# Linear attention on one core: f32 loads with the casts moved to VectorE and ScalarE, the first group on the sync queue, ten output buffers

## The chip, the cores and the metric

The kernel runs on one core of a Trainium2 chip. The metric is the device time of one execution in microseconds (us). The kernel before takes 134.85 us (median of three runs, 134.44 to 135.09). GB/s are 10^9 bytes per second, MB 10^6 bytes.

## The reference

Inputs Q, K and V are f32 arrays of 8 batches x 12 heads x 512 positions x 64 features. Per head:

```python
Q_feat = np.maximum(0, Q) + 1
K_feat = np.maximum(0, K) + 1
KV = np.einsum('bhkd,bhkv->bhdv', K_feat, V)
K_sum = np.sum(K_feat, axis=2)
numerator = np.einsum('bhqd,bhdv->bhqv', Q_feat, KV)
denominator = np.einsum('bhqd,bhd->bhq', Q_feat, K_sum)
out = numerator / (denominator[:, :, :, None] + 1e-10)
```

Each input and the output is 12.58 MB, so 37.75 MB are read and 12.58 MB written: 50.33 MB in all. Nothing is read twice.

## The kernel before, in words

The 96 heads are taken four at a time: two "pairs" (`M = 2`), each with two heads on the 128 partitions, 64 partitions to a head and eight positions (`C = 8`) to a partition. That makes `NG = 24` groups. One group is three loads (`k_raw`, `v_raw`, `q_raw`, each 128 x 1024 elements, 0.524 MB of f32 in HBM) and one store (`o_sb`, 128 x 1024 f32, 0.524 MB). In HBM each partition's share of a load is two runs of 2,048 bytes.

A group goes through three stages, each one iteration of the main loop apart:

- `features(g)`: VectorE makes `kf` from `k_raw` and `qf` from `q_raw` (add 1, then maximum with 1), ScalarE copies `v_raw` into `v_aug`, whose 65th column holds ones, so that the sum of K_feat comes out of the same matmul.
- `kv_and_transpose(g)`: 32 matmuls into `kva_ps`, eight transposes of `qf` into `qt_ps`, both taken out of PSUM by ScalarE.
- `output(g)`: 32 matmuls into two `o_ps` tiles, then for each tile a reciprocal of the denominators and a multiplication into `o_sb`, both on VectorE.

The order is written out by hand (`tc.manual_schedule()`): each engine executes its instructions in program order. Iteration `it` issues `features(it)`, `kv_and_transpose(it - 1)`, `output(it - 2)`, then `load(it + 6)` and one store. The first six groups are loaded ahead of the loop. All loads and stores are issued from GpSimd (POOL), in one order, on the software queue; each DMA there also waits for the DMA eight places before it (the compiled program uses eight completion semaphores in turn for this queue), so at most eight are in flight. The input tiles are bf16: the DMA casts f32 to bf16 on its way, which the software queue can do.

Three sizes set the waits. `IN_BUFS = 6` input buffers: `load(it + 6)` takes the buffer that `features(it)` has read. `OUT_BUFS = 7` output buffers: `output(g)` writes the buffer that the store of group g - 7 has to have left. `LAG = 5`: the store of group s stands in iteration s + 5, behind `load(s + 11)`; after the last load (group 23) there are twelve stores in a row.

Of the kernel before, what the change touches and what calls it, by code (L numbers as in the profile page):

```python
# [1 line left out]

# [5 lines left out]

FP32 = mybir.dt.float32
BF16 = mybir.dt.bfloat16  # L10
ALU = mybir.AluOpType

BANK = 512
VP = 66
IN_BUFS = 6
OUT_BUFS = 7
LAG = 5


@with_exitstack  # L20
def kernel(
    ctx: ExitStack,
    tc: tile.TileContext,
    Q: bass.AP,
    K: bass.AP,
    V: bass.AP,
    out: bass.AP,
):

    nc = tc.nc

    B, H, S, D = Q.shape
    P = 128
    C = 8
    NPAIR = B * H * S // (P * C)
    M = 2
    NG = NPAIR // M
    D1 = D + 1  # L40

    def pview(t):
        return t.flatten_outer_dims().rearrange("(n p c) d -> p n c d", p=P, c=C)

    q_dram = pview(Q)
    k_dram = pview(K)
    v_dram = pview(V)
    o_dram = pview(out)

    const = ctx.enter_context(tc.tile_pool(name="const", bufs=1))  # L50
    in_pool = ctx.enter_context(tc.tile_pool(name="in_pool", bufs=IN_BUFS))
    feat_pool = ctx.enter_context(tc.tile_pool(name="feat", bufs=3))
    mid_pool = ctx.enter_context(tc.tile_pool(name="mid", bufs=3))
    out_pool = ctx.enter_context(tc.tile_pool(name="out_pool", bufs=OUT_BUFS))
    recip_pool = ctx.enter_context(tc.tile_pool(name="recip", bufs=4))
    psum_qt = ctx.enter_context(tc.tile_pool(name="psum_qt", bufs=2, space=bass.MemoryType.PSUM))
    psum_kva = ctx.enter_context(tc.tile_pool(name="psum_kva", bufs=1, space=bass.MemoryType.PSUM))
    psum_out = ctx.enter_context(tc.tile_pool(name="psum_out", bufs=2, space=bass.MemoryType.PSUM))

    identity = const.tile([P, P], BF16, name="identity")  # L60
    NV = 3
    v_aug = [const.tile([P, M, C, VP], BF16, name=f"v_aug{i}") for i in range(NV)]

    raw = {}
    feat = {}
    mid = {}
    outs = {}

    def load(g):
        k_raw = in_pool.tile([P, M, C, D], BF16, name="k_raw")  # L70
        v_raw = in_pool.tile([P, M, C, D], BF16, name="v_raw")
        q_raw = in_pool.tile([P, M, C, D], BF16, name="q_raw")
        sl = slice(g * M, g * M + M)
        nc.gpsimd.dma_start(out=k_raw, in_=k_dram[:, sl])  # L74
        nc.gpsimd.dma_start(out=v_raw, in_=v_dram[:, sl])  # L75
        nc.gpsimd.dma_start(out=q_raw, in_=q_dram[:, sl])  # L76
        raw[g] = (k_raw, v_raw, q_raw)

    def store(g):
        nc.gpsimd.dma_start(out=o_dram[:, g * M : g * M + M], in_=outs.pop(g))  # L80

    def features(g):
        k_raw, v_raw, q_raw = raw.pop(g)
        kf = feat_pool.tile([P, M, C, D], BF16, name="kf")
        qf = feat_pool.tile([P, C, M, D], BF16, name="qf")
        nc.vector.tensor_scalar(  # L86
            out=kf, in0=k_raw, scalar1=1.0, scalar2=1.0, op0=ALU.add, op1=ALU.max
        )
        nc.scalar.copy(out=v_aug[g % NV][:, :, :, 0:D], in_=v_raw)  # L89
        nc.vector.tensor_scalar(  # L90
            out=qf.rearrange("p c m d -> p m c d"),
            in0=q_raw,
            scalar1=1.0,
            scalar2=1.0,
            op0=ALU.add,
            op1=ALU.max,
        )
        feat[g] = (kf, qf)

    def kv_and_transpose(g):  # L100
        kf, qf = feat.pop(g)
        va = v_aug[g % NV]
        kva_ps = psum_kva.tile([P, 2, BANK], FP32, name="kva_ps")
        for c in range(C):
            for m in range(M):
                for j in range(2):
                    nc.tensor.matmul(  # L107
                        kva_ps[64 * m : 64 * m + 64, j, 0:D1],
                        lhsT=kf[64 * j : 64 * j + 64, m, c, :],
                        rhs=va[64 * j : 64 * j + 64, m, c, 0:D1],  # L110
                        start=(c == 0),
                        stop=(c == C - 1),
                    )
        kva = mid_pool.tile([P, 2, VP], BF16, name="kva")
        nc.scalar.copy(out=kva[:, :, 0:D1], in_=kva_ps[:, :, 0:D1])  # L115

        qt_ps = psum_qt.tile([P, C, P], BF16, name="qt_ps")
        for c in range(C):
            nc.tensor.transpose(qt_ps[:, c, :], qf[:, c, :, :], identity)  # L119
        qt = mid_pool.tile([P, C, P], BF16, name="qt")  # L120
        nc.scalar.copy(out=qt, in_=qt_ps)  # L121
        mid[g] = (kva, qt)

    def output(g):
        kva, qt = mid.pop(g)
        o_sb = out_pool.tile([P, M, C, D], FP32, name="o_sb")
        ops = [psum_out.tile([P, 2, BANK], FP32, tag="o_ps", name="o_ps") for _ in range(M)]
        for c in range(C):
            off = (c % 4) * D1
            for m in range(M):  # L130
                for j in range(2):
                    nc.tensor.matmul(  # L132
                        ops[m][64 * j : 64 * j + 64, c // 4, off : off + D1],
                        lhsT=qt[64 * m : 64 * m + 64, c, 64 * j : 64 * j + 64],
                        rhs=kva[64 * m : 64 * m + 64, j, 0:D1],
                        start=True,
                        stop=True,
                    )
        for m in range(M):
            cells = ops[m][:, :, 0 : 4 * D1].rearrange("p b (r x) -> p b r x", x=D1)  # L140
            recip = recip_pool.tile([P, 2, 4, 1], FP32, name="recip")
            nc.vector.reciprocal(out=recip, in_=cells[:, :, :, D:D1])  # L142
            nc.vector.tensor_tensor(  # L143
                out=o_sb[:, m].rearrange("p (b r) d -> p b r d", b=2),
                in0=cells[:, :, :, 0:D],
                in1=recip.to_broadcast([P, 2, 4, D]),
                op=ALU.mult,
            )
        outs[g] = o_sb

    with tc.manual_schedule():
        for g in range(IN_BUFS):
            load(g)
            if g == 0:
                make_identity(nc, identity)
                for t in v_aug:
                    nc.gpsimd.memset(t[:, :, :, D:VP], 1.0)  # L157
        for it in range(NG + 2):
            if it < NG:
                features(it)  # L160
            if 1 <= it < NG + 1:
                kv_and_transpose(it - 1)
            if it >= 2:
                output(it - 2)
            if it + IN_BUFS < NG:
                load(it + IN_BUFS)
            s = it - 2 - (LAG - 2)
            if s >= 0:
                store(s)
        for s in range(NG + 2 - LAG, NG):  # L170
            store(s)


# [1 line left out]
_INS = ['Q', 'K', 'V']  # L175
_OUTS = [((8, 12, 512, 64), 'float32')]


# [23 lines left out]
```

## Time and profile before

| | |
|---|---|
| time, median of three | 134.85 us |
| the profiled execution | 134.27 us, its span 132.5 us |
| DMA: moved on the SBUF side of the queue | 31.46 MB (loads count as bf16) |
| DMA: read from and written to HBM | 37.75 MB and 12.58 MB |
| POOL (with DMA issue) / VectorE / TensorE / ScalarE busy | 70.3 / 57.6 / 56.6 / 53.9 us |
| one DMA issue on POOL, load or store | 0.72 to 0.73 us |
| issue to landing, median: loads / stores | 9.7 us / 9.9 us |
| SyncE (SP) | issues nothing |

The span is the time between the first and last event that the profile has; the execution's own time has 1.8 us more around it. Busy shares are averages over the whole span. A slice of the DMA row is the share of the core's 16 DMA engines that had a packet; it can be above one, because packets overlap. GB/s in the profile count bytes on the destination side: a cast load counts half of what it reads from HBM.

### The profile page before, as it was taken

The numbers are of one execution on the slowest core, as the hardware profiler recorded it, in microseconds if no ns is written. First come the engines' busy times: TensorE is split into PE (matmuls) and PEld (weight loads), VectorE is DVE, ScalarE is ACT, GpSimd is POOL, SyncE is SP. The second block draws the span as 40 slices with busy tenths as digits, with TensorE's granted clock in tenths as the row PEclk, the third lists the DMA queues.
The fourth block names the chain that finished last, engine by engine and source line by source line (L and its number), as shares of the span: only waits on it lengthen the run. The fifth ranks groups of instructions, "written<-read, shape, count | busy, mean of one in ns | idle before, by whom it ended". The sixth has DMA issues, their size and how long they took to land.

```text
span 132.5 us, 3993 instructions
## 1 busy us (share of the span) xinstructions
PE 56.6 (43%) x1728; PEld 45.5 (34%) x1728; DVE 57.6 (43%) x144; ACT 53.9 (41%) x73; POOL 70.3 (53%) x105
## 2 busy tenths in 40 slices
PE   0041576665567400516526426336065264378200
PEld 0031355454355300505415325325054153266200
DVE  0112177555567100742733724725427347297710
ACT  3035435666364463053363362461543533625000
POOL 6995546465475546555465574653554655224220
DMA  1999999999999999999999999999999999999760
GB/s 11 193 173 192 205 206 204 205 205 205 205 209 201 208 203 286 253 238 292 230 257 291 217 271 282 214 283 268 223 283 259 232 284 251 413 412 416 299 267 25
DMA packets 23057, 31.70 MB, mean 239 GB/s; under 512 B 1537, under 2 KB 19969, under 8 KB 23041
## 3 DMA queue, kind: packets, MB, share of 16 engines
q0 software_dynamic: 23040, 31.46, 110.6%
q8 instruction: 13, 0.21, 0.6%
q14 instruction: 4, 0.02, 0.0%
HBM read 37.75 MB, written 12.58 MB: 380 GB/s over the span
## 4 chain that ended last, share of the span: by engine, by line
DMA 73%; issue 11%; POOL 6%; DVE 4%; POOLq 1%; DVEq 0%
DMA out_dram<-o_sb 45%; DMA q_raw<-in_Q_dram 22%; DMA k_raw<-in_K_dram 6%; POOL out_dram L80 3%; DVE o_sb L143 3%; POOL k_raw L74 1%; POOL q_raw L76 1%; DVE qf L90 1%; POOL v_raw L75 1%; POOLq L197 1%; DVE kf L86 1%; DVE recip L142 0%; POOL identity masks.py:199 0%; POOL identity masks.py:197 0%; POOL v_aug L157 0%
## 5 line engine op out<-in xcount | busy, mean ns | idle before, releaser
L143 DVE TENSOR_TENSOR o_sb<-o_ps,recip 128x512 f32<-128x512 f32 x48 | 33.2, 692 | 42.5 <-DMA out_dram<-o_sb 41.3
L132 PE MATMUL o_ps<-kva,qt 64*64 64x65 bf16 x768 | 21.3, 244 | 46.9 <-DVE recip L142 37.9
L89 ACT COPY v_aug<-v_raw 128x1024 bf16<-128x1024 bf16 x24 | 25.1, 1046 | 26.2 <-DMA v_raw<-in_V_dram 26.2
L132 PEld LDWEIGHTS <-qt 64*64 64x64 bf16 x768 | 15.5, 149 | 55.0 <-ACT v_aug L89 31.2
L121 ACT COPY qt<-qt_ps 128x1024 bf16<-128x1024 bf16 x24 | 24.3, 1014 | 9.6 <-PE qt_ps L119 9.6
L80 POOL DMA_DIRECT2D out_dram<-o_sb x24 | 17.6, 734 | 19.4 <-DVE o_sb L143 10.2
L74 POOL DMA_DIRECT2D k_raw<-in_K_dram x24 | 17.4, 723 | 16.5 <-DMA v_raw<-in_V_dram 4.9
L107 PE MATMUL kva_ps<-v_aug,kf 64*64 64x65 bf16 x768 | 16.0, 242 | 21.3 <-ACT kva L115 12.8
L119 PE MATMUL qt_ps<-identity,qf 128*128 128x128 bf16 x192 | 24.8, 310 | 0.0
L76 POOL DMA_DIRECT2D q_raw<-in_Q_dram x24 | 17.5, 729 | 12.1 <-DMA q_raw<-in_Q_dram 6.0
L107 PEld LDWEIGHTS <-kf 64*64 64x64 bf16 x768 | 14.6, 153 | 22.5 <-issue 22.5
L75 POOL DMA_DIRECT2D v_raw<-in_V_dram x24 | 17.3, 719 | 8.9 <-DMA v_raw<-in_V_dram 4.1
L115 ACT CAST kva<-kva_ps 128x130 bf16<-128x130 f32 x24 | 6.4, 267 | 31.9 <-PE kva_ps L107 31.9
L119 PEld LDWEIGHTS <-qf 128*128 128x128 bf16 x192 | 18.5, 141 | 1.6
L90 DVE TENSOR_SCALAR qf<-q_raw 128x1024 bf16<-128x1024 bf16 x24 | 10.4, 432 | 17.7 <-DMA q_raw<-in_Q_dram 17.7
L86 DVE TENSOR_SCALAR kf<-k_raw 128x1024 bf16<-128x1024 bf16 x24 | 10.0, 418 | 6.9 <-DMA k_raw<-in_K_dram 6.9
L142 DVE RECIPROCAL recip<-o_ps 128x8 f32<-128x8 f32 x48 | 9.7, 201 | 1.9 <-PE o_ps L132 1.4
L89 ACT ACT_TABLE_LOAD x1 | 1.3, 1283 | 0.7 <-PEq L186 0.7
masks.py:199 POOL TENSOR_SCALAR_AFFINE_SELECT identity<-identity 128x128 bf16<-128x128 bf16 x1 | 0.3, 287 | 0.1
L157 POOL MEMSET v_aug<- 128x32 bf16 x3 | 0.2, 120 | 0.0
masks.py:197 POOL MEMSET identity<- 128x128 bf16 x1 | 0.2, 231 | 0.0
L186 POOL MEMSET const-float32-0.0<- 128x1 f32 x1 | 0.1, 93 | 0.3 <-issue 0.3
(3 smaller groups left out, 0.3 us busy)
## 6 DMA issues: line engine op xcount, KB each, us to landing
out_dram<-o_sb POOLq DMA_DIRECT2D x24, 512.0 KB, 9.9
k_raw<-in_K_dram POOLq DMA_DIRECT2D x24, 256.0 KB, 9.7
v_raw<-in_V_dram POOLq DMA_DIRECT2D x24, 256.0 KB, 9.7
q_raw<-in_Q_dram POOLq DMA_DIRECT2D x24, 256.0 KB, 9.7
```

Source lines behind the costliest of these rows:

```text
L74: nc.gpsimd.dma_start(out=k_raw, in_=k_dram[:, sl])
L75: nc.gpsimd.dma_start(out=v_raw, in_=v_dram[:, sl])
L76: nc.gpsimd.dma_start(out=q_raw, in_=q_dram[:, sl])
L80: nc.gpsimd.dma_start(out=o_dram[:, g * M : g * M + M], in_=outs.pop(g))
L86: nc.vector.tensor_scalar(out=kf, in0=k_raw, scalar1=1.0, scalar2=1.0, op0=ALU.add, op1=ALU.max)
L89: nc.scalar.copy(out=v_aug[g % NV][:, :, :, 0:D], in_=v_raw)
L90: nc.vector.tensor_scalar(out=qf.rearrange("p c m d -> p m c d"), in0=q_raw, scalar1=1.0, scalar2=1.0, op0=ALU.add, op1=ALU.max,)
L107: nc.tensor.matmul(kva_ps[64 * m : 64 * m + 64, j, 0:D1], lhsT=kf[64 * j : 64 * j + 64, m, c, :], rhs=va[64 * j : 64 * j + 64, m, c, 0:D1] ...
L119: nc.tensor.transpose(qt_ps[:, c, :], qf[:, c, :, :], identity)
L121: nc.scalar.copy(out=qt, in_=qt_ps)
L132: nc.tensor.matmul(ops[m][64 * j : 64 * j + 64, c // 4, off : off + D1], lhsT=qt[64 * m : 64 * m + 64, c, 64 * j : 64 * j + 64], rhs=kva[6 ...
L143: nc.vector.tensor_tensor(out=o_sb[:, m].rearrange("p (b r) d -> p b r d", b=2), in0=cells[:, :, :, 0:D], in1=recip.to_broadcast([P, 2, 4, ...
```

## The change

Input tiles become f32, so that the loads no longer cast; the two VectorE instructions and the ScalarE copy of `features` read f32 and write bf16 as before, with unchanged code. Group 0 gets three f32 tiles of its own in a new pool (`head_pool`) and its loads are issued from SyncE (`nc.sync`, a hardware queue); all other loads and all stores remain on GpSimd. The masks and the ones columns, which GpSimd makes after the loads of group 0, are now made after the loads of group 1. There are ten output buffers in place of seven, and `LAG` goes from 5 to 3: the store of group s stands in iteration s + 3, behind `load(s + 9)`, and ten stores follow the last load.

```diff
-OUT_BUFS = 7
-LAG = 5
+OUT_BUFS = 10
+LAG = 3
...
+    head_pool = ctx.enter_context(tc.tile_pool(name="head_pool", bufs=1))
...
     def load(g):
-        k_raw = in_pool.tile([P, M, C, D], BF16, name="k_raw")
-        v_raw = in_pool.tile([P, M, C, D], BF16, name="v_raw")
-        q_raw = in_pool.tile([P, M, C, D], BF16, name="q_raw")
+        if g == 0:
+            pool, dt, eng = head_pool, FP32, nc.sync
+        else:
+            pool, dt, eng = in_pool, FP32, nc.gpsimd
+        k_raw = pool.tile([P, M, C, D], dt, name="k_raw")
+        v_raw = pool.tile([P, M, C, D], dt, name="v_raw")
+        q_raw = pool.tile([P, M, C, D], dt, name="q_raw")
         sl = slice(g * M, g * M + M)
-        nc.gpsimd.dma_start(out=k_raw, in_=k_dram[:, sl])
-        nc.gpsimd.dma_start(out=v_raw, in_=v_dram[:, sl])
-        nc.gpsimd.dma_start(out=q_raw, in_=q_dram[:, sl])
+        eng.dma_start(out=k_raw, in_=k_dram[:, sl])
+        eng.dma_start(out=v_raw, in_=v_dram[:, sl])
+        eng.dma_start(out=q_raw, in_=q_dram[:, sl])
         raw[g] = (k_raw, v_raw, q_raw)
...
         for g in range(IN_BUFS):
             load(g)
-            if g == 0:
+            if g == 1:
                 make_identity(nc, identity)
```

## The prediction

> **What bounds the kernel now.** I read the slices of the page first. The DMA row and the GB/s below it, and the traffic to HBM:
>
> ```profile
> DMA  1999999999999999999999999999999999999760
> GB/s 11 193 173 192 205 206 204 205 205 205 205 209 201 208 203 286 253 238 292 230 257 291 217 271 282 214 283 268 223 283 259 232 284 251 413 412 416 299 267 25
> ...
> HBM read 37.75 MB, written 12.58 MB: 380 GB/s over the span
> ```
>
> The DMA engines are full from the second slice to the 37th; no compute engine is busy over half of the span. The GB/s row has three levels, and a finer look at three quiet windows (us, busy times by engine, clock, DMA share, GB/s) gives them:
>
> ```profile
> core 0: us, PE busy (x) PEld busy (x) DVE busy (x) ACT busy (x) POOL busy (x), PEclk, DMA share, GB/s
> 14.00:40.00 26.00, 15.51 (x472) 12.16 (x471) 14.60 (x38) 14.04 (x21) 14.58 (x20) 1.00 1.24 205
> 66.00:96.00 30.00, 12.74 (x370) 10.18 (x368) 13.26 (x33) 13.35 (x18) 16.66 (x24) 1.00 1.19 257
> 114.00:122.00 8.00, 5.19 (x176) 4.28 (x176) 6.25 (x15) 3.92 (x6) 1.64 (x3) 1.00 1.03 415
> ```
>
> The first window holds loads alone; a cast load counts half its HBM bytes, so 205 is 410 GB/s read. The second mixes three loads and a store per group: 2.097 MB in HBM against 1.311 MB counted, so 257 x 1.6 = 411. The third is stores alone, f32 on both sides: 415. Three levels in the row are thus one speed of HBM bytes, 410 to 415 GB/s. 50.33 MB at 412 are 122 us of the 132.5; about 10 us lie at the ends. The waits show the same from the compute side:
>
> ```profile
> DVE o_sb L143 <- DMA out_dram<-o_sb: 41.3, 13, 8.7
> PE o_ps L132 <- DVE recip L142: 37.9, 14, 8.5
> ```
>
> VectorE waits 41.3 us for an output buffer that a store still holds, and TensorE waits behind it. While the queue is full this costs nothing. It does matter once the loads end, because compute is then three groups in arrears:
>
> ```profile
> 112.91 0.72 POOL L80 DMA_DIRECT2D out_dram<-o_sb  x1 [0.20 <-issue]
> 116.85 0.73 POOL L80 DMA_DIRECT2D out_dram<-o_sb  x1 [3.22 <-DVE o_sb L143]
> ...
> 124.29 0.72 POOL L80 DMA_DIRECT2D out_dram<-o_sb  x1 [1.76 <-DVE o_sb L143]
> 126.77 0.72 POOL L80 DMA_DIRECT2D out_dram<-o_sb  x1 [1.75 <-DVE o_sb L143]
> ```
>
> The last five stores leave 2.48 us apart, VectorE's pace, where a store needs 0.524 MB / 415 = 1.26 us. The windows at both ends show what is lost:
>
> ```profile
> 2.50:3.00 0.50, 0.00 (x0) 0.00 (x0) 0.00 (x0) 0.00 (x0) 0.50 (x2) 1.00 0.31 29
> 3.00:3.50 0.50, 0.00 (x0) 0.00 (x0) 0.00 (x0) 0.00 (x0) 0.50 (x1) 1.00 0.92 96
> 3.50:4.00 0.50, 0.00 (x0) 0.00 (x0) 0.00 (x0) 0.00 (x0) 0.42 (x3) 1.00 1.19 199
> ...
> 124.00:125.00 1.00, 0.65 (x30) 0.51 (x30) 0.27 (x2) 0.00 (x0) 0.71 (x1) 1.00 0.72 283
> 127.00:128.00 1.00, 0.00 (x0) 0.00 (x0) 0.00 (x0) 0.00 (x0) 0.50 (x1) 1.00 0.04 16
> ```
>
> By 4.0 us the queue has moved 0.5 x (29 + 96 + 199) = 162 kB, worth 0.8 us at 205, so it starts in effect at 3.2 us. At 127 to 128 us it stands empty, one store still to come.
>
> [...] The trace shows 1.27 (issue) to some 3 us for the first, which includes 0.84 us of issue; of SP it has nothing. [...] in the trace POOL's issue stays at 0.71 to 0.82 us.
>
> **The change part by part.**
>
> *f32 loads.* HBM bytes don't change. SBUF takes 37.75 MB in place of 18.87. No row shows an f32 load. The nearest is the f32 store, 415 against 410 for the cast load; if loads come to 415 too, 37.75 MB take 91.0 us in place of 92.1, a gain of 1.1. The other bound: writing SBUF at twice the rate costs something, say 395 GB/s, 95.6 us, +3.5. I take half of the gain, **-0.5**, because the direction of the store differs.
>
> *Casts.* The rows concerned:
>
> ```profile
> L90 DVE TENSOR_SCALAR qf<-q_raw 128x1024 bf16<-128x1024 bf16 x24 | 10.4, 432 | 17.7 <-DMA q_raw<-in_Q_dram 17.7
> L86 DVE TENSOR_SCALAR kf<-k_raw 128x1024 bf16<-128x1024 bf16 x24 | 10.0, 418 | 6.9 <-DMA k_raw<-in_K_dram 6.9
> ```
>
> [...] +0.27 each, 48 x 0.27 = +13 us of VectorE. The ScalarE copy stays at 1.05 [...]. VectorE's iteration goes from 2.48 us to 3.0, hidden under the transfers of a group: 2.097 MB / 411 = 5.1 us with stores, 1.573 / 410 = 3.84 us without. So **0**. [...]
>
> *Group 0 on SP.* Three issues leave POOL and go to SP, which has nothing else to do. POOL's first load, now of group 1, still leaves at 1.27 and would arrive as before, so the worst is 0. [...] I take **-0.9**. Three fewer DMAs pass through the eight-deep window. The masks, about 0.8 us on POOL, again follow three issues, so `identity` is ready at the same time, before the first transpose (9.0 us).
>
> *Ten output buffers and LAG 3.* `output(g)` now needs the store of group g - 10, placed in iteration g - 7, nine iterations earlier; before, store g - 7 in iteration g - 2, four earlier. At 5.1 us an iteration nine exceed the 9.9 us that a store is in flight by far, so the 41.3 us wait goes, and compute follows the landing loads. What is late next is the loads: harmless, as the queue is full. The store of group s stands behind the load of q for group s + 9, which waits for `qf` of group s + 3; VectorE does that after `o_sb` of group s. So the earlier store adds no wait on POOL, and the loads behind it aren't held up.
>
> At the end: let T be the landing of q_raw of group 23. Stores 14 to 20 are ready, 7 x 1.26 = 8.8 us of transfer. VectorE still owes groups 21 to 23: `qf` 0.7, then two reciprocals and two multiplications, 1.75, so 21 is ready at T + 2.4; 22 follows at about T + 4.2 and 23, behind transposes (1.04), ScalarE (1.01) and matmuls, at about T + 6.5. The queue needs them from T + 8.8 on. It never runs dry. Before, the store of group 12 had landed when VectorE went on at 115.02; eleven were left, 5.77 MB, 13.9 us at 415: 128.9. The last really landed at 126.77 + 3.2 (the shortest issue-to-landing of a store) = 130.0. So **-1.1**. The close after it, 132.5 - 130.0 = 2.5 us, stays.
>
> *Sum:* -0.5 + 0 - 0.9 - 1.1 = -2.5: a span of 130.0, 131.8 us for an execution like the profiled one (134.27), which is 0.6 below the median; set against the median of 134.85, **132.3 us**.
>
> **The rivals.**
>
> *A (0.60):* the sum above, 132.3; its own range 130.5 to 133.9.
>
> *B (0.22), the other side:* f32 loads are slower, since SBUF is written at twice the rate. For it: no transfer in this trace writes SBUF above 210 GB/s. Against it: stores move 415 through the same engines. The ends are worth 2.0 us, so it decides where 92.1 us of loads become 94.1, below 401 GB/s; at 395 the time is 134.85 + 3.5 - 2.0 = 136.3. A third of this case lies within 0.5%.
>
> *C (0.13):* only the tail is saved: SP's first packets come no earlier, or share the engines with GpSimd's such that the head's dips (174 and 150 GB/s between 6 and 9 us) grow; loads run at 410. 134.85 - 1.1 = 133.8. Two thirds of it still count as faster.
>
> *D (0.05):* VectorE becomes the bound. [...]
>
> **How the numbers follow.** Changes under 0.5% can't be told from none. Faster: A, and 0.09 of C: 0.69. Same: 0.04 of C, 0.07 of B, 0.02 of D: 0.13. Slower: 0.15 of B and 0.03 of D: 0.18. The range, 130.0 to 136.0, takes in the lower end of A with loads a little above 415, and B down to about 396 GB/s.
>
> **What would show it.** Right: load-only windows near 415 GB/s counted in f32; no wait of the multiplication on a store; `kf` and `qf` at 0.69; a first `kf` about 1 us before 5.11; DMA share near one until the last store, which leaves before the queue is dry. Wrong: load-only windows below 400, stores leaving 2.5 us or more apart at the end, or POOL issues well over 0.8 us with DMA gaps after them.

## The result and the profile after

The changed kernel takes 136.15 us (median of four runs, 135.90 to 136.72) against 134.81 for the kernel before: a ratio of 1.011, 95% interval 1.006 to 1.015. It is slower, by 1.3 us, where 2.5 us of gain was forecast, and 136.15 lies just outside the range.

The slices of the changed kernel, its hardware and software queues, and the traffic to HBM:

```profile
DMA  3999999999999999999999999999999999999960
GB/s 114 385 395 387 387 385 386 385 383 386 386 382 390 399 401 396 403 402 403 403 397 403 398 404 407 393 403 405 398 399 410 397 402 407 398 413 412 386 276 12
...
q0 software_dynamic: 13392, 48.76, 93.4%
q1 hardware_dynamic: 816, 1.57, 3.2%
...
HBM read 37.75 MB, written 12.58 MB: 375 GB/s over the span
```

The engines are still full from end to end, but now every byte counts once, and the row reads directly in HBM bytes. There is no level at 410 to 415 until the stores stand alone, in the slices with 413 and 412; the prediction's own sign of being wrong, load-only windows below 400, is there. Two windows, loads alone and loads mixed with stores (us, busy times by engine, clock, DMA share, GB/s):

```profile
14.00:34.00 20.00, 12.82 (x383) 10.39 (x372) 13.54 (x28) 11.35 (x16) 10.61 (x15) 1.00 1.02 385
66.00:96.00 30.00, 14.85 (x426) 11.96 (x429) 17.48 (x36) 12.76 (x18) 16.84 (x23) 1.00 1.02 401
```

385 stands where the kernel before read 410, and 401 where it moved 411. Ten load-only groups of 1.573 MB cost 10 x (1.573/385 - 1.573/410) = 2.5 us more, fourteen mixed groups of 2.097 MB 14 x (2.097/401 - 2.097/411) = 1.8 us more: an estimate of 4.3 us lost (setting two kernels against each other, below, gives 3.7). The waits and the casts came out as forecast. The waits of VectorE and ScalarE:

```profile
ACT v_aug L95 <- DMA v_raw<-in_V_dram: 66.6, 24, 4.8
DVE qf L96 <- DMA q_raw<-in_Q_dram: 42.9, 23, 6.9
```

Compute waits for landing loads now; a wait of the multiplication on a store's buffer, 41.3 us before, isn't in the list any more. The casts cost what was forecast:

```profile
L96 DVE TENSOR_SCALAR qf<-q_raw 128x1024 bf16<-128x1024 f32 x24 | 16.7, 694 | 42.9 <-DMA q_raw<-in_Q_dram 42.9
L92 DVE TENSOR_SCALAR kf<-k_raw 128x1024 bf16<-128x1024 f32 x24 | 17.2, 716 | 8.6 <-DMA k_raw<-in_K_dram 8.6
```

### The profile page after: what moved, and what is told of

Same layout as the page of the kernel before. It is cut to its first block, busy times and chain, and to the rows that moved or that the text cites. A ratio compares the mean times of both kernels' runs of the same rounds, so it can differ in the third digit from the quotient of the medians.

```text
span 134.2 us, 3988 instructions
## 1 busy us (share of the span) xinstructions
PE 60.3 (45%) x1728; PEld 48.7 (36%) x1728; DVE 72.0 (54%) x144; ACT 52.5 (39%) x73; POOL 68.9 (51%) x102
## 4 chain that ended last, share of the span: by engine, by line
DMA 83%; issue 9%; POOL 2%; DVE 1%; POOLq 1%
DMA q_raw<-in_Q_dram 68%; DMA k_raw<-in_K_dram 8%; DMA v_raw<-in_V_dram 7%; POOL out_dram L86 1%; POOL k_raw L80 1%; POOLq L203 1%; DVE qf L96 1%; DVE o_sb L149 1%; DVE recip L148 0%; POOLq L82 0%; POOLq L86 0%; POOLq L192 0%
## 5 line engine op out<-in xcount | busy, mean ns | idle before, releaser
L95 ACT CAST v_aug<-v_raw 128x1024 bf16<-128x1024 f32 x24 | 25.1, 1045 | 66.6 <-DMA v_raw<-in_V_dram 66.6
L96 DVE TENSOR_SCALAR qf<-q_raw 128x1024 bf16<-128x1024 f32 x24 | 16.7, 694 | 42.9 <-DMA q_raw<-in_Q_dram 42.9
L80 POOL DMA_DIRECT2D k_raw<-in_K_dram x23 | 16.9, 734 | 18.7 <-DMA k_raw<-in_K_dram 8.0
L82 POOL DMA_DIRECT2D q_raw<-in_Q_dram x23 | 16.7, 724 | 12.5 <-DMA q_raw<-in_Q_dram 7.1
L92 DVE TENSOR_SCALAR kf<-k_raw 128x1024 bf16<-128x1024 f32 x24 | 17.2, 716 | 8.6 <-DMA k_raw<-in_K_dram 8.6
```

What stands on the lines that cost most here:

```text
L80: eng.dma_start(out=k_raw, in_=k_dram[:, sl])
L82: eng.dma_start(out=q_raw, in_=q_dram[:, sl])
L92: nc.vector.tensor_scalar(out=kf, in0=k_raw, scalar1=1.0, scalar2=1.0, op0=ALU.add, op1=ALU.max)
L96: nc.vector.tensor_scalar(out=qf.rearrange("p c m d -> p m c d"), in0=q_raw, scalar1=1.0, scalar2=1.0, op0=ALU.add, op1=ALU.max,)
```

## Experiments: which part of the change loses

The theory at this point: the f32 loads are the whole loss, and the other parts gain (the "load theory"). The rival: something else costs, such as the earlier stores among the loads (the "order theory"). Four kernels ran beside the kernel before, which took 134.71 us with them.

**Ten output buffers and LAG 3 alone.**

```diff
-OUT_BUFS = 7
-LAG = 5
+OUT_BUFS = 10
+LAG = 3
```

> The kernel before with ten output buffers and LAG 3 only; loads cast as before. Load theory (f32 loads are the whole loss, the buffers help): the tail's 1.1 us are saved, 133.7 us, load-only windows at 410 GB/s of HBM reads. Order theory (the loss comes from stores that stand earlier among the loads): slower than before, 135.5 us or more, with mixed windows below 411.

133.86 us, ratio 0.9935 (0.9914 to 0.9956): 0.85 us gained. Load-only windows stay at 205 GB/s counted (410 read), mixed ones at 257:

```profile
14.00:34.00 20.00, 11.79 (x361) 9.39 (x359) 10.74 (x28) 10.46 (x15) 10.48 (x15) 1.00 1.24 205
66.00:96.00 30.00, 13.93 (x400) 11.50 (x398) 13.97 (x34) 11.00 (x17) 16.19 (x23) 1.00 1.19 257
```

The order theory falls.

**The changed kernel with cast loads put back** for groups 1 to 23; group 0 stays f32 on SyncE.

```diff
-            pool, dt, eng = in_pool, FP32, nc.gpsimd
+            pool, dt, eng = in_pool, BF16, nc.gpsimd
```

> The changed kernel with the loads of groups 1 to 23 cast to bf16 again; group 0 stays f32 on SyncE, ten output buffers, LAG 3. Load theory: head (0.8 to 0.9 us) and tail (1.1 us) are gained and nothing is lost, 132.9 us. Order theory, or a theory that the second queue costs: no better than 134.8 us.

132.43 us, ratio 0.9829 (0.9788 to 0.9869). So head and tail together gain 2.3 us, and the f32 loads of groups 1 to 23 lose 136.15 - 132.43 = 3.7.

**f32 input tiles alone**, in the order of the kernel before.

```diff
-        k_raw = in_pool.tile([P, M, C, D], BF16, name="k_raw")
+        k_raw = in_pool.tile([P, M, C, D], FP32, name="k_raw")
```

(and the same for `v_raw` and `q_raw`)

> The kernel before with f32 input tiles only; all loads on GpSimd, seven output buffers, LAG 5. Load theory: load-only windows at 385 GB/s as in the changed kernel, mixed ones at 401; it lacks the head's and the tail's gain, so 138 us. Order theory: the same as before, 134.8 us.

140.0 us, ratio 1.038 (1.034 to 1.042), with load-only windows at 386 and mixed ones at 400 as the load theory says:

```profile
14.00:34.00 20.00, 11.62 (x328) 9.31 (x328) 12.64 (x25) 8.81 (x13) 9.54 (x14) 1.00 1.02 386
66.00:96.00 30.00, 14.52 (x427) 11.23 (x428) 18.02 (x36) 13.12 (x18) 16.65 (x23) 1.00 1.02 400
```

It is 2 us above the 138 expected. The first three of the last five stores show where some of it lies (issues on POOL; start, us, what it had waited for):

```profile
122.03 1.04 POOL L80 DMA_DIRECT2D out_dram<-o_sb  x1 [3.25 <-DVE o_sb L143]
124.91 1.04 POOL L80 DMA_DIRECT2D out_dram<-o_sb  x1 [1.84 <-DVE o_sb L143]
127.79 0.72 POOL L80 DMA_DIRECT2D out_dram<-o_sb  x1 [1.84 <-DVE o_sb L143]
```

They leave 2.88 us apart, where they left 2.48 apart before; the last two follow at 2.48 again. With seven buffers compute is in arrears when the loads end, the queue runs dry (266 GB/s from 126 to 127 us, 127 from 128 to 129), and VectorE's longer casts (0.72 and 0.78 us on average, before 0.42 and 0.43) come onto the path. That is 0.8 us; the rest of the 2 wasn't traced. In the changed kernel, with ten buffers, compute follows the loads closely, and the last three stores leave 2.48 us apart.

**All loads on SyncE's hardware queue, f32.**

```diff
-            pool, dt, eng = in_pool, FP32, nc.gpsimd
+            pool, dt, eng = in_pool, FP32, nc.sync
```

> The changed kernel with all loads on SyncE's hardware queue, f32; stores stay on GpSimd. If it is the software queue's way of issuing f32 loads that is slow: load-only windows at 405 to 415 GB/s and 132 to 133 us. If an f32 write into SBUF is slow whatever the queue (direction or packet size): windows at 385 again and 135.5 to 136.5 us.

141.78 us (median of three runs; a fourth took 143.86), ratio 1.052 (1.046 to 1.058): neither forecast. The rate is not much better before the first store goes out at 18.9 us:

```profile
8.00:16.00 8.00, 3.31 (x80) 2.60 (x80) 2.78 (x4) 3.23 (x5) 0.00 (x0) 1.00 1.05 392
```

392 GB/s, with packets half as large (256 to a load in place of 128). So moving the loads off the software queue, and to smaller packets, doesn't bring the rate back. From 122 us on the engines of this run are about half empty (123 to 246 GB/s by slices) while groups still land 5 us apart; why stays open.

## Experiments: why an f32 load is slow

Next to be told apart: the write into SBUF at full rate, two HBM runs in one packet, or the compute beside it. The next four kernels only load and store, and each ran once: f32 loads, casting loads, f32 loads from one HBM run of 4,096 bytes, and loads that widen 16 to 32 bits. Each of 72 loads is touched by a VectorE copy of one element per partition, and 24 stores of one constant tile follow.

```python
for i, t in enumerate(raw.pop(g)):
    nc.vector.tensor_copy(out=seen[:, g, i : i + 1], in_=t[:, 0, 0, 0:1])
```

> Only the 72 loads, f32 on GpSimd's queue with 2,048-byte runs in HBM, each tile touched by one VectorE copy of one element per partition; then 24 stores of one constant tile. The attention itself is left out. If the f32 load is slow by itself: load windows at 385 GB/s, as in the changed kernel. [...]

> The same with bf16 tiles, the DMA casting; the attention is left out. 205 GB/s counted at the destination, 410 of HBM reads, if the cast load is faster by itself; the load phase then is 6 us shorter than with f32 tiles. If the difference comes from compute: no difference.

> The f32 loads alone with each partition's 4,096 bytes in one run of HBM in place of two of 2,048 (each partition gets other rows; the attention is left out). If two HBM runs in one packet slow the f32 load: 405 or more. If it is the write into SBUF: 385 again.

> Loads alone that read half of the bytes (16-bit integers, 1,024 of each 2,048 bytes) and write 32-bit integers, so SBUF takes the full 0.524 MB per load and HBM gives half; the attention is left out. If the write into SBUF is the limit: 380 to 390 GB/s at the destination although HBM reads fall to 193. If the read of HBM in large packets is the limit: clearly above 400 at the destination.

The same window of each in that order (us, VectorE and POOL busy, clock, DMA share, GB/s at the destination):

```profile
14.00:90.00 76.00, 9.24 (x60) 41.76 (x58) 1.00 1.03 417
```

```profile
14.00:90.00 76.00, 9.08 (x59) 41.11 (x58) 1.00 1.24 205
```

```profile
14.00:90.00 76.00, 9.27 (x61) 30.64 (x58) 1.00 1.03 420
```

```profile
14.00:90.00 76.00, 9.22 (x60) 40.68 (x57) 1.00 1.47 414
```

Plain f32 loads alone run at 417, faster than the cast loads' 410, and the first store leaves 1.4 us earlier than with cast loads (95.97 against 97.33), where a slow f32 load would have made it some 6 us *later*. The write into SBUF takes 414 to 420 (so the write theory falls), and one HBM run of 4,096 bytes is hardly better than two of 2,048 (420 against 417).

Taken as planned, this left the compute theory: something on VectorE, ScalarE or TensorE slows the loads. But in the changed kernel's load-only phase the rate doesn't follow the engines. Cut into 48 windows of half a microsecond from 12 to 36 us, a least-squares fit of GB/s on the busy shares gives -4 ± 5 for VectorE, -2 ± 4 for ScalarE, -2 ± 5 for TensorE. The compute theory needed some 30 GB/s from them.

One thing had changed unnoticed between the two kernels: where the input tiles start in SBUF. In the compiled programs, the input tiles of the kernels before and after start at byte 23104 of each partition and whole multiples of 2,048 or 4,096 further on (three `v_aug` tiles of 2,112 bytes each stand ahead of them). 23104 is 45 x 512 + 64. In the loads-only kernels they start at 20992 = 41 x 512. So the new theory was the address, and both kernels were tried the other way round.

**The changed kernel with its input tiles moved by 448 bytes**, to 23552 = 46 x 512 (64 bytes more, behind them, keep the output tiles' offset of 416 from a multiple of 512):

```diff
     identity = const.tile([P, P], BF16, name="identity")
+    const.tile([P, 112], FP32, name="pad_in")
...
+    pad_pool = ctx.enter_context(tc.tile_pool(name="pad_pool", bufs=1))
+    pad_pool.tile([P, 16], FP32, name="pad_out")
     out_pool = ctx.enter_context(tc.tile_pool(name="out_pool", bufs=OUT_BUFS))
```

> The changed kernel with 448 unused bytes per partition ahead of the input tiles, so that these start at a multiple of 512 bytes in SBUF (23552 and on) in place of 64 beyond one (23104 and on); the output tiles keep their 416 beyond a multiple of 512. Address theory [...]: load-only windows at 415 to 417 GB/s, as with the loads alone (those tiles started at a multiple of 512), and 131 to 132.5 us. Compute theory (the engines' work beside the loads slows them): 385 GB/s and 136.1 us as in the changed kernel.

**The loads alone with their tiles moved by 64 bytes**, to 21056:

> The f32 loads alone again, with 64 unused bytes ahead of the input tiles, so that they start 64 beyond a multiple of 512; the attention is left out. Address theory: 385 GB/s. Compute theory: 417, as with the loads alone before.

First the load-only window of the changed kernel with moved tiles, then the loads alone with moved tiles:

```profile
14.00:34.00 20.00, 13.22 (x393) 10.72 (x393) 14.57 (x30) 11.01 (x16) 11.21 (x16) 1.00 1.02 414
```

```profile
14.00:90.00 76.00, 8.54 (x57) 40.44 (x56) 1.00 1.02 387
```

Both rates turn over. The full kernel goes from 385 to 414 with all its compute in place; the loads alone fall from 417 to 387 with none, and with nothing moved but its input tiles. The compute theory falls. The padded kernel takes 132.03 us (130.99 to 132.43), ratio to the kernel before 0.9815 (0.9782 to 0.9848): 512 unused bytes turn a change that loses 1.3 us into one that gains some 2.5. Its slices hold one level throughout:

```profile
GB/s 106 407 398 420 423 406 421 415 412 418 408 422 404 413 413 412 413 415 417 410 417 411 416 418 410 418 417 410 417 416 416 410 421 410 416 413 412 387 260 5
```

**Which side and which loads mind.** Two more kernels ran with these: output tiles aligned too, and cast loads with all tiles aligned.

```diff
-    pad_pool.tile([P, 16], FP32, name="pad_out")
+    pad_pool.tile([P, 40], FP32, name="pad_out")
```

> As the run with aligned input tiles, and the output tiles too start at a multiple of 512. If reading SBUF off a multiple costs as writing might: stores go from 413 to 420 or more and 0.5 us are gained on that run. If reads don't mind: the same as that run.

> The changed kernel with cast loads for groups 1 to 23 (132.4 us), input and output tiles both at multiples of 512 bytes. Address theory: a cast load writes half of the bytes[...]: 205 GB/s at the destination as before, no gain from the inputs; within 0.5 us of 132.4, so that aligned f32 loads at 417 match or beat it. Compute theory: no change either.

132.52 us (ratio 0.9827, 0.9784 to 0.9871) and 132.87 (0.9864, 0.9809 to 0.9919). Output tiles at a multiple of 512 gain nothing over an offset of 416: both run at 414 in load-only and at 415 in mixed windows. The trace also records how long each packet took: a store's, from 118 to 122 us, a median of 160 ns at either offset. So a store, which reads SBUF, shows no such cost. Aligned cast loads show 205 as before, and a median of 98 ns a packet with and without the offset, so a cast load doesn't show it either. The padded f32 kernel, the cast one at 132.43 and these two overlap in their intervals; which is best can't be told.

**Which multiple counts.** The loads alone, at three more offsets, one run each.

```diff
     seen = const.tile([P, NG, 4], FP32, name="seen")
+    const.tile([P, 8], FP32, name="pad_in")     # 32 or 64 in place of 8 for 128 and 256 bytes
```

> The f32 loads alone (the attention is left out), input tiles 32 bytes beyond a multiple of 512. [...] A cost that depends on being off a multiple of 64: below 387.

> The same at 128 beyond a multiple of 512. If tiles must start at a multiple of 256 or 512 bytes: 387 GB/s. If 128 is enough: 417.

> The same at 256 beyond a multiple of 512. [...] If 256 is enough: 417.

At 32, then at 128, then at 256:

```profile
14.00:90.00 76.00, 8.52 (x57) 40.45 (x56) 1.00 1.02 387
```

```profile
14.00:90.00 76.00, 8.46 (x55) 40.05 (x56) 1.00 1.03 387
```

```profile
14.00:90.00 76.00, 9.23 (x60) 41.99 (x58) 1.00 1.03 417
```

256 is as good as 0; 32, 64 and 128 cost the same. Of the five offsets run, the two that are multiples of 256 bytes give 417 and the three others 387: a step, not a slope. By these rates the step is 7.7%. The packets say the same: 4,096 bytes take a median of 159 to 160 ns on a multiple of 256 and 173 ns at each of the three other offsets, 13 ns more; in the load-only windows of the full kernels it is 173 (changed) and 159 (padded).

**Whether SyncE's queue minds.** The traces of the full kernels tell. Group 0's packets, 2,048 bytes each, have the engines to themselves until GpSimd's first packet at 4.9 us. Up to 4.7 us they take a median of 84 ns in the changed kernel, at an offset of 64, and 84 ns in the padded one, at 0. From 3 to 4 us that is 401 GB/s at 64, and 408 and 401 in the two f32 kernels with aligned input tiles. So no step shows there, and the kernel with all loads on SyncE was slow for another reason: its packets, too, take 84 ns, and 16 engines at 2,048 bytes in 84 ns come to 390 GB/s, near its 392. That kernel with aligned tiles wasn't run. Whether the queue or the size of its packets makes the difference is open.

The runs show the step, its place and where it is absent. Why a packet of an f32 load on GpSimd's queue takes 13 ns more stays open.

## Why the prediction was wrong

*f32 loads, -0.5.* This is the step that failed. It took half of a gain from the nearest row, the f32 store at 415. The term measured +3.7 us (136.15 against 132.43 with cast loads), with load-only windows at 385. Aligned, the rate read from the store would have held: 414 in the full kernel, and 132.03 us against 132.43, a difference within the noise. What it left out is that a store reads SBUF from an offset of 416 without harm (160 ns a packet there and at 0), while an f32 load on GpSimd's queue writes SBUF, where the tiles' start counts (173 ns a packet at an offset of 64, 159 to 160 at 0). The offset could have been known: the compiled program places `identity` at byte 16512, and it and three tiles of 2,112 bytes take 6,592. That the offset matters could not be seen in the trace of the kernel before, whose cast loads run at 410 on a multiple or off it.

*Rival B* (f32 loads slower, ends still gained) had the right place and the right sign, and its price was close: +3.5 for a load rate of 395, which the author assumed, against 3.7 measured, -2.0 for the ends against -2.3, 136.3 us in all. Its reason, that SBUF is written at twice the rate, was wrong: SBUF takes 417. That its price came out so close is luck. It got 0.22.

*Casts, 0.* Right in the changed kernel: 0.69 and 0.72 us against the 0.69 forecast, hidden under the transfers. The 0.69 was the author's estimate, the time of the 128x512 f32 multiplication in the trace of before (692 ns; less the 0.42 us of the bf16 instruction, the +0.27); that an f32 `kf` or `qf` would take as long, no row of that trace showed. Nor did one show an f32 input that makes VectorE the bound (rival D): in the changed kernel VectorE is busy for 54% of the span. With f32 tiles alone, in the old order, they are not wholly hidden, as the two gaps of 2.88 us between stores show.

*Group 0 on SP, -0.9.* Right in kind. The size was the author's estimate: SyncE issues nothing in the kernel before, so its trace showed no packet from there. The first `kf` starts at 4.26 us, before at 5.11. Between the kernels with and without it, both with cast loads and ten buffers, 133.86 and 132.43, it is 1.4 us. By 4.0 us the queue has moved 645 kB (before: 324 kB of HBM reads), which is 0.8 us. The packets of those two kernels, counted in HBM bytes, show where the rest comes from: the one with group 0 on SyncE leads by 0.38 MB (0.9 us) at 4 us and by 0.68 MB (1.7 us) at 10 us, and keeps that to the end of the loads. Most of the second part is won from 6 to 8 us, where the kernel without it moves 0.52 MB and this one 0.76. The early dip that rival C feared would grow became smaller: the lowest rate over a whole microsecond from 4 to 10 us is 356 GB/s in the changed kernel, and was 150 counted, 300 read, before.

*Ten buffers and LAG 3, -1.1.* Right in kind, -0.85 alone. The working at the tail held in the main: the last q_raw landed at T = 119.2, and the last three stores left at T + 2.7, T + 5.2 and T + 7.7 (forecast 2.4, 4.2, 6.5), each before T + 8.8. "It never runs dry" was a little too much: VectorE's pace of 2.48 us stays between these stores, and from 127 to 128 us, while the last one is being issued, the DMA share falls to 0.68.

The three measured terms, -1.4, -0.85 and +3.7, come from kernels that each add one part to the last, so that they add up to the whole difference by construction; their sum of +1.45 is no further evidence.

## What to carry to other kernels

When a DMA-bound kernel moves plain data into SBUF from GpSimd's queue, look at where its tiles start: 256-byte multiples were worth 7.7% of the load rate here (417 GB/s against 387), and a small tile allocated ahead of them can shift all, as 64 bytes did in the loads alone. A transfer type that the trace doesn't show can't be priced with confidence by one that differs in direction; the bound on its cost, here +3.5 us, has to weigh in the chance. And when a part is measured by itself, check what else the smaller kernel changed: the loads-only run pointed at compute until the address was held fixed.

## What the runs showed of the hardware that was not expected

- f32 loads issued from GpSimd (packets of 4,096 bytes) into SBUF tiles that start off a multiple of 256 bytes run at 387 GB/s at offsets of 32, 64 and 128 alike, at 417 on a multiple (0 and 256): 173 ns a packet against 159 to 160. Stores from SBUF (offset 416 or 0) and casting loads to bf16 (offset 64 or 0) show no difference.
- f32 loads issued from SyncE (packets of 2,048 bytes) show no difference between offsets of 64 and 0 either: 84 ns a packet.
- An aligned plain f32 load is a little faster than a casting one, 417 against 410 GB/s of HBM reads (one run each), though it writes twice the bytes into SBUF.
- A load that widens 16 to 32 bits reads 207 GB/s from HBM and still gives 414 GB/s at the destination, no more than a plain one (417). So the read of HBM, which reaches 410 to 420 in the other loads-only runs with tiles on a multiple of 512, doesn't set its pace; what does wasn't tried.
- 24 stores of one and the same tile ran at 360 to 366 GB/s where stores of different tiles run at 413 to 415. Why was not tried.
